# Hybrid decoder layer: the mixer's last convolution tile taken ahead of the recurrence's input, eight of its taps on ScalarE and GpSimd, gating and output products by channel halves

## The chip, the cores and the metric

The kernel runs on one core of a Trainium2 chip. The metric is the device time of one execution in microseconds (us). A core has five engines that work side by side and meet through semaphores: TensorE (PE, matrix products into PSUM, with PEld its weight loads), VectorE (DVE), ScalarE (ACT), GpSimd (POOL) and SyncE (SP, which issues most DMAs). Each works through its own queue in order.

## The reference

One decoder layer for 512 tokens of width 1024, all in float32. A half step of a SwiGLU network stands on either side of a token mixer:

```python
x = x + 0.5 * ffn1(rmsnorm(x))
x = x + mixer(rmsnorm(x))
x = x + 0.5 * ffn2(rmsnorm(x))
return rmsnorm(x)
```

The mixer makes four parts of 512 channels from one projection. Two of them feed a convolution branch, two a linear recurrence, and one output projection takes both:

```python
c_val, c_gate, r_x, r_gate = split(h @ w_in)
u  = silu(layernorm(depthwise_conv(c_val * sigmoid(c_gate), width=31)))
xr = depthwise_conv(r_x, width=4)
r, i = sigmoid(blockdiag(xr, w_a)), sigmoid(blockdiag(xr, w_x))
a  = exp(-8 * r * softplus(-lam))
y  = scan(a, sqrt(1 - a * a) * i * xr) * gelu(r_gate)      # h[t] = a[t] h[t-1] + b[t]
return concat([u, y]) @ w_out
```

## The kernel before

Every product is made of three in a fast 32-bit format: each operand is split into a high and a low part, and high x high, high x low and low x high are added in PSUM. So a product of 128 output channels for 512 tokens over a width of 1024 is 24 matmuls of 128x512 (`mm_feat`, L294).

The program is written as a list of units (`Unit`, L66): slabs of weights, a piece of TensorE work (`mm`), and what empties its accumulators (`evac`). `run` (L239) walks the list, loads and splits the slabs a few units ahead, issues `mm`, advances side work by an estimate of the time passed, and issues `evac`. Side work stands in generators: `chains` (norms, the recurrence `lru`, `layernorm`), `convs` (convolution taps on VectorE) and `pool_convs` (on ScalarE and GpSimd). `need(key)` advances them until a result is there. The tile framework then orders each engine's queue by priority and program order; `tc.keep_in_program_order` (called `pin` here) fixes an instruction's place.

The mixer's 512 channels per part are four tiles of 128 on the partitions, with the tokens along the free dimension. Its units on TensorE, in order:

- `zc_units(c)` for convolution tiles 0, 1 and 2 (gate product, value product; the sigmoid and the multiplication leave the input in `ub`),
- `rx_units`: the recurrence's input, four tiles; `evac` makes the four-tap convolution on ScalarE and VectorE (L728 to L733), the last one starts `lru`,
- `zc_units(3)`, then `rg_units`: the recurrence's gate branch, four tiles, emptied by a GELU (L755) that asks for the key `roots` first,
- `out_units`: the output projection. It first takes the recurrence's half y (slabs `sy`; t is a tile of 128 tokens) for t = 0, 1, 2, asks for the LayerNorm's variance (`need("var")`), takes y for t = 3, and then the convolution's half u (slabs `su`).

A convolution tile has 31 taps. Tiles 0, 2 and 3 are on VectorE (`conv_dve`, L642): one instruction per tap, alternately into two PSUM banks, and an add of the two at the end. Tile 1 is on ScalarE, which makes a scaled copy per tap, and GpSimd, which adds the copies in pairs (`conv_pool`, L662). When a tile is done, TensorE sums it over the channels with a matrix of ones (`channel_sum`, L629, into `pm`); after the fourth, `layernorm` subtracts the mean, squares (ScalarE), sums again on TensorE, takes root and reciprocal, and makes SiLU and the split of u.

`lru` (L765): eight block-diagonal gate products on TensorE (L771, into `pga`), eight sigmoids (L772), GpSimd multiplies input by gate (L777), ScalarE makes tanh, exp and squares (L781 to L786), VectorE combines (L789), ScalarE takes the root (L793), GpSimd multiplies it in (L794), VectorE scans the four tiles (L801). Then it waits until all four GELU tiles are there and no VectorE convolution is left (L804), multiplies y by the gate in two halves of two tiles (L808), and splits it (L809, L810); `done["y"]` lets the output products start.

ScalarE's activation functions sit in tables; a switch between some of them puts an `ACT_TABLE_LOAD` into its queue. Weights of the following network are split by ScalarE (`S.copy`, L202) into one of five `hl` buffers, where the slabs `sy` lay before.

Of the kernel before, what the change touches and what calls it, by code (L numbers as in the profile page):

```python
# [29 lines left out]
TAPS = 31  # L30
PR_NORM = 800
# [40 lines left out]
def layer_kernel(ctx: ExitStack, tc, x, gains, w_g1, w_u1, w_d1a, w_d1b, w_in,  # L72
# [519 lines left out]
    def zc_units(c, parts):  # L592
# [12 lines left out]
        def val_out(t0, n):  # L605
            V.tensor_mul(mx["ub"][:, c, 30 + t0:30 + t0 + n], box["v"][:, :n], box["s"][:, :n])
# [35 lines left out]
    def conv_dve(c):  # L642
        acc, o = [bank("pc"), bank("pc")], conv_out(c)
        for j in range(TAPS):
# [7 lines left out]
            else:  # L652
                V.scalar_tensor_tensor(out=o if j == TAPS - 2 else to, in0=src,  # L653
# [3 lines left out]
        V.tensor_add(o, acc[0], o)  # L657
        yield 0.66
        conv_done(c)


    def conv_pool(c):  # L662
# [16 lines left out]
        conv_done(c)  # L679

    def layernorm():
# [33 lines left out]
        done["u"] = (hi, lo)  # L715
# [28 lines left out]
    def rg_units():  # L744
# [7 lines left out]
        def evac(c):  # L752
# [3 lines left out]
            if c == 3:  # L756
                done["gl"] = True
# [7 lines left out]
    def lru():  # L765
        xr, r, i_, th = lr["xr"], two("r"), two("i"), two("th")
        for c in range(4):
            at = (slice(None), c % 2, slice(None))
            for gi, (to, b) in enumerate(((r, P_BA), (i_, P_BX))):
                pga = bank("pga")  # L770
                PE.matmul(pga, bd[:, gi, c, :], xr[c // 2][at], start=True, stop=True)  # L771
# [3 lines left out]
        pin = tc.keep_in_program_order  # L775
# [3 lines left out]
        for c in range(4):  # L779
            at = (slice(None), c % 2, slice(None))  # L780
            S.activation(th[c // 2][at], r[c // 2][at], AF.Tanh, scale=psp[:, c:c + 1])  # L781
        for c in range(4):
            at = (slice(None), c % 2, slice(None))
            S.activation(r[c // 2][at], r[c // 2][at], AF.Exp, scale=nsp[:, c:c + 1])
# [14 lines left out]
        for c in range(4):  # L799
            at = (slice(None), c % 2, slice(None))  # L800
            pin(V.tensor_tensor_scan(th[c // 2][at], r[c // 2][at], xr[c // 2][at],  # L801
                                     0.0, ALU.mult, ALU.add))
# [4 lines left out]
        for q in range(2):  # L807
            pin(V.tensor_mul(th[q], th[q], lr["gl"][q]))  # L808
            S.copy(hi[q], th[q])  # L809
            V.tensor_sub(lo[q], th[q], hi[q].bitcast(F32))  # L810
            dve(2.4)
        done["y"] = (hi, lo)


    def out_units(after):
# [13 lines left out]
        def part(ts, slabs, key, first, cs=range(4), halves=(0, 1)):  # L829
            hi, lo = need(key)  # L830
            for t in ts if first else ():
                box[t] = [bank("po") for _ in range(2)]
            for t in ts:
                for oh in halves:
                    for c in cs:
                        at = (slice(None), c % 2, toks(t))
# [253 lines left out]
```

## Time and profile before

| | before |
|---|---|
| three runs, median (lowest to highest) | 880.58 us (879.61 to 880.58) |
| the profiled execution, its own time | 884.38 us |
| its span | 882.4 us |
| busy in the span: PE, PEld | 853.7 us, 767.0 us |
| DVE, ACT, POOL | 612.5, 413.3, 90.0 us |
| granted TensorE clock, mean | 0.989 |
| mixer in the span: its first input product, first output product on y, on u | 368.29, 476.98, 505.52 us |

The profile is one execution under the hardware profiler, with times from the start of its span; it took 3.8 us longer than the median of the runs. A row of a timeline has the start, the duration, the engine, the source line, the operation, output tile<-input tiles, shape and count, and in brackets the idle time before it with what ended it. A float32 product of ones shows as two matmul records for one instruction. The ends of matmuls are modelled.

### The profile page before, as it was taken

How to read it: one execution, taken by the hardware profiler on the slowest of the kernel's cores; microseconds unless marked ns; L12 is line 12 of the kernel's file. 1: busy time of each engine (PE TensorE's matmuls, PEld its weight loads, DVE VectorE, ACT ScalarE, POOL GpSimd, SP SyncE). 2: the span in 40 equal slices, each digit the busy share in tenths (PEclk: the TensorE clock that was granted, in tenths of full speed). 3: DMA queues.
4: the chain of work that ended last, by engine and by line, in shares of the span. 5: the costliest groups of instructions: out<-in, count | busy, mean ns of one | idle time of the engine just before them, and what ended most of it. 6: DMA issues, size and time to landing. Idle time of an engine off the chain costs nothing.

```text
span 882.4 us, 13317 instructions
## 1 busy us (share of the span) xinstructions
PE 853.7 (97%) x5388; PEld 767.0 (87%) x5388; DVE 612.5 (69%) x854; ACT 413.3 (47%) x647; POOL 90.0 (10%) x112
## 2 busy tenths in 40 slices
PE   7999998999998999999996999999999999999996
PEld 5999987999888998898783789999889999899985
DVE  5999665987667863659988569587547775558644
ACT  7666433646434652426652535455225554235523
POOL 2000011000011001208830010000000000000001
PEclk9999999999999999999997999999999999999999
DMA  7543688364788389655442021234312324223402
GB/s 280 166 168 106 233 286 311 139 215 167 228 306 301 97 268 404 234 214 192 143 151 88 4 92 64 82 105 131 123 49 97 127 89 164 76 72 97 143 1 95
DMA packets 36719, 139.10 MB, mean 158 GB/s; under 512 B 5041, under 2 KB 5169, under 8 KB 33970
## 3 DMA queue, kind: packets, MB, share of 16 engines
q1 hardware_dynamic: 29170, 112.04, 37.8%
q0 software_dynamic: 6912, 25.17, 7.2%
q10 hardware_dynamic: 576, 1.05, 0.3%
q8 instruction: 42, 0.69, 0.3%
q14 instruction: 19, 0.16, 0.1%
HBM read 110.98 MB, written 27.26 MB: 157 GB/s over the span
## 4 chain that ended last, share of the span: by engine, by line
PE 70%; issue 15%; DVE 5%; DMA 5%; ACT 4%; POOL 1%; SPq 0%; POOLq 0%; ACTq 0%; DVEq 0%
PE px L308 17%; PE pz L308 8%; PE pz L299 7%; PE pd L515 5%; PE pd L516 5%; PE pd L514 5%; PE pgate L299 5%; PE pup L299 5%; PE pw L308 4%; DVE pc L653 2%; DMA sraw<-in_w_out 2%; DMA raw<-in_w_u 2%; PE po L514 1%; PE po L516 1%; PE po L515 1%
## 5 line engine op out<-in xcount | busy, mean ns | idle before, releaser
L211 DVE TENSOR_TENSOR hl<-raw,hl 128x1024 fp32r<-128x1024 f32 (+1 forms) x132 | 142.5, 1083 | 58.3 <-ACT hl L202 44.1
L514 PE MATMUL pd<-hl,act 128*128 128x512 f32 x304 | 118.5, 390 | 0.0
L515 PE MATMUL pd<-hl,act 128*128 128x512 f32 x304 | 118.4, 389 | 0.0
L516 PE MATMUL pd<-hl,act 128*128 128x512 f32 x304 | 118.3, 389 | 0.0
L308 PE MATMUL px<-sx,hl 128*128 128x256 f32 x816 | 108.4, 283 | 5.6 <-ACT sg L467 5.6
L211 DVE TENSOR_TENSOR hl<-tt,hl 128x1024 fp32r<-128x1024 f32 x68 | 82.9, 1219 | 38.5 <-ACT hl L237 37.1
L308 PEld LDWEIGHTS px<-sx,hl 128*128 128x128 f32 x816 | 101.7, 192 | 6.2 <-ACT sg L467 6.2
L308 PE MATMUL pz<-sx,hl 128*128 128x256 f32 x816 | 106.1, 279 | 0.0
L308 PEld LDWEIGHTS pz<-sx,hl 128*128 128x128 f32 x816 | 99.8, 189 | 0.0
L202 ACT CAST hl<-raw 128x1024 fp32r<-128x1024 f32 x64 | 66.5, 1053 | 63.1 <-PE pd L516 47.7
L308 PE MATMUL px<-h_hi,hl 128*128 128x256 f32 x544 | 85.6, 280 | 0.0
L237 ACT CAST hl<-tt 128x1024 fp32r<-128x1024 f32 x68 | 71.6, 1053 | 28.7 <-PE pd L516 18.4
L237 ACT CAST hl<-raw 128x1024 fp32r<-128x1024 f32 x68 | 56.8, 836 | 41.0 <-PE pd L516 29.2
L308 PEld LDWEIGHTS px<-h_hi,hl 128*128 128x128 f32 x544 | 74.2, 188 | 1.2
L516 PEld LDWEIGHTS pd<-hl,act 128*128 128x128 f32 x304 | 57.1, 188 | 11.9
L514 PEld LDWEIGHTS pd<-hl,act 128*128 128x128 f32 x304 | 57.1, 188 | 11.6
L515 PEld LDWEIGHTS pd<-hl,act 128*128 128x128 f32 x304 | 57.1, 188 | 11.5
L299 PE MATMUL pz<-h_hi,hl 128*128 128x512 f32 (+1 forms) x320 | 64.9, 352 | 0.0
L299 PEld LDWEIGHTS pz<-h_hi,hl 128*128 128x128 f32 x320 | 51.8, 188 | 9.2 <-issue 1.9
L653 DVE SCALAR_TENSOR_TENSOR pc<-sx,ch,pc 128x512 f32<-128x512 f32 x84 | 56.9, 749 | 0.0
L288 DVE TENSOR_TENSOR slo<-sraw,shi 128x1024 fp32r<-128x1024 f32 x24 | 29.4, 1223 | 36.0 <-ACT shi L287 36.0
L287 ACT CAST shi<-sraw 128x1024 fp32r<-128x1024 f32 x24 | 25.2, 1051 | 53.4 <-DMA sraw<-in_w_in 32.3
(181 smaller groups left out, 1397.5 us busy)
## 6 DMA issues: line engine op xcount, KB each, us to landing
raw<-in_w_g SPq DMA_DIRECT2D x44, 512.0 KB, 3.5
raw<-in_w_u SPq DMA_DIRECT2D x44, 512.0 KB, 3.8
hl<-wsi SPq DMA_DIRECT2D x16, 1024.0 KB, 4.8
sraw<-in_w_in SPq DMA_DIRECT2D x16, 512.0 KB, 5.8
wsi<-shi POOLq DMA_DIRECT2D x16, 512.0 KB, 5.5
wsi<-slo POOLq DMA_DIRECT2D x16, 512.0 KB, 5.6
raw<-in_w_d1a SPq DMA_DIRECT2D x16, 512.0 KB, 3.6
raw<-in_w_d2a SPq DMA_DIRECT2D x16, 512.0 KB, 3.5
```

Source lines behind the costliest of these rows:

```text
L202: S.copy(s.hi, s.raw)
L211: V.tensor_sub(s.lo, s.raw, s.hi.bitcast(F32))
L237: S.copy(s.hi, s.raw)
L287: S.copy(hi, raw)
L288: V.tensor_sub(lo, raw, hi.bitcast(F32))
L299: PE.matmul(ps, w[:, k, :], h[:, k, t0:t0 + n], start=(i == 0 and k == 0), stop=(i == 2 and k == KT - 1))
L308: PE.matmul(ps[:, 0:HT], w[:, k * P:(k + 1) * P], h[:, k, :], start=(first and i == 0 and k == 0), stop=(i == 2 and k == 3), skip_group_ch ...
L514: PE.matmul(ps, ahi, whi, start=first, stop=False)
L515: PE.matmul(ps, ahi, wlo, start=False, stop=False)
L516: PE.matmul(ps, alo, whi, start=False, stop=last)
L653: V.scalar_tensor_tensor(out=o if j == TAPS - 2 else to, in0=src, scalar=par(c, P_DW + j), in1=to, op0=ALU.mult, op1=ALU.add)
```

## The change

Four things change, all in the mixer.

1. The units of tile 3 of the convolution (`zc_units(3)`) stand before `rx_units` and no longer behind them.
2. Tile 3's last eight taps (23 to 30) leave VectorE. `conv_part` makes eight scaled copies on ScalarE and four adds on GpSimd; `conv_dve` makes 23 taps, waits for the key `part`, and adds that sum.
3. The recurrence scans, gates and splits its output by halves of two channel tiles. The gate of a half needs only that half's GELU tiles (`gl0`, `gl1`), and the condition that no convolution is left is gone. Sigmoids, tanhs and exps are pinned in program order, the subtraction that makes the low part too.
4. The output products on y for t = 0, 1, 2 come by halves: first tiles 0 and 1 for the three t, then tiles 2 and 3. Their keys are `y0`, `y1`, and `u0`, `u1` for the other branch.

```diff
-                else:
-                    convs.append(conv_dve(c))
+                elif c == 3:
+                    pool_convs.append(conv_part(c, range(TAPS - PART, TAPS)))
+                    convs.append(conv_dve(c, TAPS - PART, "part"))
+                else:
+                    convs.append(conv_dve(c, TAPS))
...
-        V.tensor_add(o, acc[0], o)
+        V.tensor_add(o, acc[taps % 2], o)
         yield 0.66
+        if rest is not None:
+            while rest not in done:
+                yield 0.3
+            V.tensor_add(o, o, done[rest])
+            yield 0.66
         conv_done(c)
...
+    def conv_part(c, taps):
+        acc = slot([P, 2, T], "ca")
+        for j in taps[::2]:
+            to = acc if j == taps[0] else slot([P, 2, T], "cm")
+            for i in range(2):
+                S.activation(to[:, i, :], mx["ub"][:, c, j + i:j + i + T], AF.Copy,
+                             scale=par(c, P_DW + j + i))
+            if j > taps[0]:
+                G.tensor_add(acc, acc, to)
+                yield 2.5
+        G.tensor_add(acc[:, 0, :], acc[:, 0, :], acc[:, 1, :])
+        yield 1.25
+        done["part"] = acc[:, 0, :]
...
-                S.activation(to[c // 2][at], pga, AF.Sigmoid, bias=par(c, b))
+                pin(S.activation(to[c // 2][at], pga, AF.Sigmoid, bias=par(c, b)))
...
-        for c in range(4):
-            at = (slice(None), c % 2, slice(None))
-            pin(V.tensor_tensor_scan(th[c // 2][at], r[c // 2][at], xr[c // 2][at],
-                                     0.0, ALU.mult, ALU.add))
-            dve(1.2)
-        while "gl" not in done or convs:
-            yield 1
         hi, lo = two("yhi", F32R), two("ylo", F32R)
         for q in range(2):
+            for c in range(2):
+                at = (slice(None), c, slice(None))
+                pin(V.tensor_tensor_scan(th[q][at], r[q][at], xr[q][at], 0.0, ALU.mult, ALU.add))
+                dve(1.2)
+            yield 1
+        for q in range(2):
+            while f"gl{q}" not in done:
+                yield 1
             pin(V.tensor_mul(th[q], th[q], lr["gl"][q]))
             S.copy(hi[q], th[q])
-            V.tensor_sub(lo[q], th[q], hi[q].bitcast(F32))
+            pin(V.tensor_sub(lo[q], th[q], hi[q].bitcast(F32)))
             dve(2.4)
-        done["y"] = (hi, lo)
+            done[f"y{q}"] = (hi[q], lo[q])
...
-        out_ = [Unit(sy, 5.44, lambda t=t: part((t,), sy, "y", True)) for t in range(3)]
+        out_ = [Unit(sy[2 * q:2 * q + 2], 2.72, lambda q=q, t=t: part((t,), sy, True, (2 * q, 2 * q + 1)))
+                for q in range(2) for t in range(3)]
...
-    u += rx_units() + zc_units(3, [ALL]) + rg_units()
+    u += zc_units(3, [ALL]) + rx_units() + rg_units()
```

What the framework made of it stands in the queues. In the rows below a name has its tile's number behind it, a line number is that of the kernel concerned, and `x8` counts equal instructions.

TensorE, where the gate products stand before: the last of them, then tile 3's value product (`pz_4372`), then the first product of the gate branch (`pz_4425`) with the sum of tile 1 (`pm_4180<-cv_3963`) near its end.

```order
L771 MATMUL pga_4358<-xr_4105,bd 128x512
L299 MATMUL pz_4372<-h_hi,hl_4152 128x512 x8
L299 MATMUL pz_4372<-h_lo,hl_4152 128x512 x8
L299 MATMUL pz_4372<-h_hi,hl_4152 128x512 x8
L299 MATMUL pz_4425<-h_hi,hl_4204 128x512 x8
L299 MATMUL pz_4425<-h_lo,hl_4204 128x512 x8
L299 MATMUL pz_4425<-h_hi,hl_4204 128x512 x6
L633 MATMUL pm_4180<-cv_3963,ones 128x512
```

TensorE in the changed kernel: the last matmuls of the third recurrence input, the fourth (`pz_4349`), the sum of tile 1, the first product of the gate branch (`pz_4398`), and then the gate products (`pga_4429` on).

```order
L300 MATMUL pz_4298<-h_hi,hl_4102 128x512 x8
L300 MATMUL pz_4349<-h_hi,hl_4146 128x512 x8
L300 MATMUL pz_4349<-h_lo,hl_4146 128x512 x8
L300 MATMUL pz_4349<-h_hi,hl_4146 128x512 x8
L637 MATMUL pm_4174<-cv_3963,ones 128x512
L300 MATMUL pz_4398<-h_hi,hl_4196 128x512 x8
L300 MATMUL pz_4398<-h_lo,hl_4196 128x512 x8
L300 MATMUL pz_4398<-h_hi,hl_4196 128x512 x8
L797 MATMUL pga_4429<-xr_4198,bd 128x512
```

The gate products moved behind one more product and behind the sum of tile 1, which stood behind them.

VectorE before: the end of tile 2 (`cv_4184`), tile 3's input (L606), the recurrence's pair of combinations (L789), and then tile 3's first tap.

```order
L657 TENSOR_TENSOR cv_4184<-pc_4182,cv_4184 128x512
L606 TENSOR_TENSOR sx_464_3727<-pz_4372,sgc_4368 128x512
L789 SCALAR_TENSOR_TENSOR th_4331<-i_4329,th_4331 128x1024
L789 SCALAR_TENSOR_TENSOR th_4332<-i_4330,th_4332 128x1024
L647 TENSOR_SCALAR pc_4487<-sx_464_3727,ch 128x512
```

VectorE in the changed kernel, at that pair (L814): thirteen taps of tile 3 (`pc_4457`, `pc_4458`) stand ahead of it, the last two of which are shown, and ten behind it; then come the scans (L828), the first half's gating (L834), and the two adds that end tile 3 (L661, L666).

```order
L657 SCALAR_TENSOR_TENSOR pc_4458<-sx_464_3727,ch,pc_4458 128x512
L657 SCALAR_TENSOR_TENSOR pc_4457<-sx_464_3727,ch,pc_4457 128x512
L814 SCALAR_TENSOR_TENSOR th_4427<-i_4425,th_4427 128x1024
L814 SCALAR_TENSOR_TENSOR th_4428<-i_4426,th_4428 128x1024
L657 SCALAR_TENSOR_TENSOR pc_4458<-sx_464_3727,ch,pc_4458 128x512
...
L828 SCALAR_TENSOR_TENSOR th_4427<-r_4423,xr_4198 128x512 x2
L828 SCALAR_TENSOR_TENSOR th_4428<-r_4424,xr_4199 128x512 x2
L834 TENSOR_TENSOR th_4427<-th_4427,gl_4396 128x1024
L661 TENSOR_TENSOR cv_4178<-pc_4458,cv_4178 128x512
L666 TENSOR_TENSOR cv_4178<-cv_4178,ca_4334 128x512
```

The pair moved from ahead of tile 3 to its middle, and the first half's gating from behind tile 3's last add to ahead of it.

ScalarE before, in LayerNorm: the root of the variance (L696), the table for SiLU, SiLU and cast of u (L707, L708), and then the first cast of the following network's weights (L202).

```order
L696 ACTIVATE rs_4660<-pm_4645,lneps 128x512
L707 ACT_TABLE_LOAD
L707 ACTIVATE cv_3963<-cv_3963,ch 128x256 x2
L708 CAST uhi_4688<-cv_3963 128x256 x2
L707 ACTIVATE cv_4184<-cv_4184,ch 128x256 x2
L708 CAST uhi_4689<-cv_4184 128x256 x2
...
L202 CAST hl_4802<-raw_4568 128x1024
```

ScalarE in the changed kernel, at the same place.

```order
L720 ACTIVATE rs_4709<-pm_4682,lneps 128x512
L203 CAST hl_4811<-raw_4594 128x1024
L203 CAST hl_4813<-raw_4596 128x1024
L203 CAST hl_4815<-raw_4655 128x1024
L731 ACT_TABLE_LOAD
L731 ACTIVATE cv_3963<-cv_3963,ch 128x256 x2
L732 CAST uhi_4723<-cv_3963 128x256 x2
```

Three casts of weights moved from behind u to ahead of it. TensorE's sum of tile 3 moved too: before, it stood ahead of the first output product; now it stands behind 68 of the 72 products on y for t = 0, 1, 2, with the variance sums right behind those, ahead of y for t = 3.

More of the change, by code (lines that the diff above doesn't have):

```diff
@@ L30 @@
 TAPS = 31
+PART = 8
 PR_NORM = 800
@@ L639, in conv_done, with conv_dve @@
             chains.append((PR_LN, layernorm()))
-    def conv_dve(c):
+    def conv_dve(c, taps, rest=None):
         acc, o = [bank("pc"), bank("pc")], conv_out(c)
-        for j in range(TAPS):
+        for j in range(taps):
             src, to = mx["ub"][:, c, j:j + T], acc[j % 2]
@@ L652, in conv_dve @@
             else:
-                V.scalar_tensor_tensor(out=o if j == TAPS - 2 else to, in0=src,
+                V.scalar_tensor_tensor(out=o if j == taps - 1 else to, in0=src,
                                        scalar=par(c, P_DW + j), in1=to,
@@ L714, in layernorm @@
             dve(1.6)
-        done["u"] = (hi, lo)
+        for q in range(2):
+            done[f"u{q}"] = (hi[q], lo[q])
     lr = {}
@@ L755, in evac @@
                 S.activation(lr["gl"][c // 2][:, c % 2, :], lr["g", c], AF.Gelu_apprx_tanh))
-            if c == 3:
-                done["gl"] = True
+            if c % 2:
+                done[f"gl{c // 2}"] = True
         out_ = []
@@ L780, in lru @@
             at = (slice(None), c % 2, slice(None))
[L781 removed]
+            pin(S.activation(th[c // 2][at], r[c // 2][at], AF.Tanh, scale=psp[:, c:c + 1]))
         for c in range(4):
             at = (slice(None), c % 2, slice(None))
[L784 removed]
+            pin(S.activation(r[c // 2][at], r[c // 2][at], AF.Exp, scale=nsp[:, c:c + 1]))
         for q in range(2):
@@ L827, in out_units, with part @@
         box = {}
-        def part(ts, slabs, key, first, cs=range(4), halves=(0, 1)):
-            hi, lo = need(key)
-            for t in ts if first else ():
+        def part(ts, slabs, first, cs=range(4), halves=(0, 1)):
+            for t in ts if first and cs[0] == 0 else ():
                 box[t] = [bank("po") for _ in range(2)]
@@ L835, in part @@
                     for c in cs:
+                        hi, lo = need(f"{'y' if first else 'u'}{c // 2}")
                         at = (slice(None), c % 2, toks(t))
-                        mm_tok(box[t][oh], hi[c // 2][at], lo[c // 2][at],
+                        mm_tok(box[t][oh], hi[at], lo[at],
                                slabs[c].hi[:, cols(oh)], slabs[c].lo[:, cols(oh)],
@@ L849, in fin_two @@
                     fin(t, oh)
-        out_ = [Unit(sy, 5.44, lambda t=t: part((t,), sy, "y", True)) for t in range(3)]
+        out_ = [Unit(sy[2 * q:2 * q + 2], 2.72, lambda q=q, t=t: part((t,), sy, True, (2 * q, 2 * q + 1)))
+                for q in range(2) for t in range(3)]
         out_ += [Unit([], 0.0, lambda: need("var"))]
-        out_ += [Unit(sy, 5.44, lambda: part((3,), sy, "y", True))]
-        out_ += [Unit(su, 2.72, lambda c=c: part((0, 1), su, "u", False, (c,)),
+        out_ += [Unit(sy, 5.44, lambda: part((3,), sy, True))]
+        out_ += [Unit(su, 2.72, lambda c=c: part((0, 1), su, False, (c,)),
                       fin_two if c == 3 else None) for c in range(4)]
-        out_ += [Unit(su, 2.72, lambda t=t, oh=oh: part((t,), su, "u", False, halves=(oh,)),
+        out_ += [Unit(su, 2.72, lambda t=t, oh=oh: part((t,), su, False, halves=(oh,)),
                       lambda t=t, oh=oh: fin(t, oh)) for t in (2, 3) for oh in range(2)]
```

3 lines of the change are left out of this document (2 added, 1 removed).

## The prediction

> **What bounds the kernel now.** I read the profile's page, then TensorE's timeline through the mixer, the clock by windows, and the timelines of the engines that TensorE waits for there.
>
> ```profile
> span 882.4 us, 13317 instructions
> PE 853.7 (97%) x5388; PEld 767.0 (87%) x5388; DVE 612.5 (69%) x854; ACT 413.3 (47%) x647; POOL 90.0 (10%) x112
> ```
>
> TensorE (PE) is busy for 97% of the span, so a change in the mixer is worth what it does to holes in TensorE's row and to its clock. The timeline (start, duration, engine, line, operation, count, in brackets the idle time before and who ended it):
>
> ```profile
> 431.68 7.03 PE L771 MATMUL pga<-xr,bd 128*128 128x512 f32 x16
> 438.14 2.40 PE L299 MATMUL pz<-h_hi,hl 128*128 128x512 f32 x8
> 449.00 1.02 PE L633 MATMUL pm<-cv,ones 128*128 128x512 f32 x2
> 466.68 1.04 PE L299 MATMUL pz<-h_hi,hl 128*128 128x512 f32 x2
> 474.77 2.08 PE L633 MATMUL pm<-cv,ones 128*128 128x512 f32 x2 [7.06 <-DVE cv L657]
> 476.98 0.80 PE L514 MATMUL po<-hl,yhi 128*128 128x512 f32 x1
> 482.90 0.50 PE L514 MATMUL po<-hl,yhi 128*128 128x512 f32 x1 [0.96 <-ACT yhi L809]
> 483.71 3.60 PE L633 MATMUL pm<-sq,ones 128*128 128x512 f32 x8
> 487.38 0.40 PE L514 MATMUL po<-hl,yhi 128*128 128x512 f32 x1
> 505.52 0.39 PE L514 MATMUL po<-hl,uhi 128*128 128x512 f32 x1
> ```
>
> The input products end at 467.7 and the first output product (L514) starts at 476.98: one hole of 9.3 us with a lone sum (L633) in it, then 0.96 us at 482.90. From 487.38 on there is no hole: 80 products to 505.52, 0.227 us each. The windows (PE's granted clock stands ahead of the DMA share, third from the right) show what the hole does to the clock:
>
> ```profile
> 468.00:471.00 3.00, 0.00 (x0) 0.00 (x0) 3.00 (x6) 0.34 (x1) 0.00 (x0) 0.99 0.78 235
> 471.00:475.00 4.00, 0.23 (x1) 0.23 (x2) 3.97 (x7) 0.00 (x0) 0.00 (x0) 0.50 0.21 86
> 479.00:480.80 1.80, 1.80 (x6) 1.43 (x5) 1.80 (x4) 0.00 (x0) 0.00 (x0) 0.50 0.00 0
> 480.80:482.00 1.20, 1.14 (x4) 0.57 (x3) 0.91 (x1) 0.20 (x1) 0.00 (x0) 0.84 0.00 0
> ```
>
> It halves about 3.3 us after the last product and is whole again at about 481.2, so the products from 476.98 to 481.2 lose half of 4.2 us, 2.1 us. All that could be won here is 9.3 - 0.9 (the sum, at 0.9 of full speed) + 1.0 + 2.1 = 11.5 us. What ends the hole is VectorE (DVE):
>
> ```profile
> 444.28 0.69 DVE L606 TENSOR_TENSOR sx<-pz,sgc 128x512 f32<-128x512 f32 x1 [2.50 <-PE pz L299]
> 446.24 2.36 DVE L789 SCALAR_TENSOR_TENSOR th<-i,th 128x1024 f32<-128x1024 f32 x2 [1.27 <-ACT i L786]
> 453.83 5.03 DVE L801 TENSOR_TENSOR_SCAN th<-r,xr 128x512 f32<-128x512 f32 x4
> 458.79 13.89 DVE L653 SCALAR_TENSOR_TENSOR pc<-sx,ch,pc 128x512 f32<-128x512 f32 x21
> 474.03 0.69 DVE L657 TENSOR_TENSOR cv<-pc,cv 128x512 f32<-128x512 f32 x1
> 474.63 1.22 DVE L808 TENSOR_TENSOR th<-th,gl 128x1024 f32<-128x1024 f32 x1
> ```
>
> A tap costs 13.89 / 21 = 0.66 us. Channel tile 3 gets its input only at 444.28, and its taps fill VectorE until the gating (L808).
>
> **The change part by part.** *Tile 3 ahead, eight taps away, gates later.* VectorE loses 8 x 0.66 = 5.3 us and gains one add of 0.6 us, and tile 3's input comes 30 us earlier. But the four recurrence inputs and their gate products (L771) now come later on TensorE. Three products of 24 matmuls each take 16.38 us, one 5.46:
>
> ```profile
> 415.46 16.38 PE pz L299 x72
> ```
>
> At 431.68, where the gate products stood, the fourth recurrence input begins and ends at 437.1. Behind it the order has the sum of tile 1 (before: at 449.00, amid a later product), which needs GpSimd's last add:
>
> ```profile
> 429.13 8.64 POOL L675 TENSOR_TENSOR ca<-ca,cm 128x1024 f32<-128x1024 f32 x4 [3.10 <-ACT cm L673]
> 437.85 1.29 POOL L677 TENSOR_TENSOR cv<-ca 128x512 f32<-128x512 f32 x1
> ```
>
> GpSimd waits there for copies that ScalarE (ACT) makes behind an evacuation at 426.49 (below); the evacuation at that place of the new order ends the same product by count, so 439.1 stands and TensorE waits 2.0 us. With the sum (0.9) and one product the gate products start at 445.6, 13.9 later than 431.68. That is the price of the new order, and it meets this chain on ScalarE:
>
> ```profile
> 426.49 0.75 ACT L728 ACTIVATE px<-pz,ch 128x512 f32<-128x512 f32 x1 [3.00 <-PE pz L299]
> 427.64 2.57 ACT L673 ACTIVATE cm<-sx,ch 128x512 f32<-128x512 f32 x4
> 439.43 1.95 ACT L781 ACTIVATE th<-r,psp 128x512 f32<-128x512 f32 x3
> 441.40 1.28 ACT L784 ACT_TABLE_LOAD   x1
> 445.16 2.00 ACT L786 ACTIVATE i<-r 128x1024 f32<-128x1024 f32 x2
> 475.88 1.04 ACT L809 CAST yhi<-th 128x1024 fp32r<-128x1024 f32 x1 [7.54 <-DVE th L808]
> 487.35 0.69 ACT L696 ACTIVATE rs<-pm,lneps 128x512 f32<-128x512 f32 x1 [1.10 <-PE pm L633]
> 491.79 1.28 ACT L707 ACT_TABLE_LOAD   x1 [3.75 <-DVE cv L706]
> 493.09 1.10 ACT L707 ACTIVATE cv<-cv,ch 128x256 f32<-128x256 f32 x2
> 494.09 0.70 ACT L708 CAST uhi<-cv 128x256 fp32r<-128x256 f32 x2
> 503.68 3.90 ACT L202 CAST hl<-raw 128x1024 fp32r<-128x1024 f32 x4 [4.09 <-PE po L516]
> ```
>
> From gate products to VectorE's first L789 it takes 446.24 - 431.68 = 14.6 us (sigmoids, tanh, table load, exp, squares), the pair done at 448.6. Sigmoids pinned ahead of all tanhs add 0 to 0.6 (one 0.65 tanh stood in a gap). So the pair runs from 460.4 to 462.8. In VectorE's new order ten of tile 3's 23 taps stand behind it. The thirteen ahead of it are 8.6 us of work after tile 2. That one ends at about 444: VectorE's queue has tile 3's input behind tile 2's first tap, so all else of tile 2 waits some 3 us for that product, which ends near 415 (the row at 415.46 begins behind it); 30 taps and 12 recurrence taps follow, 42 x 0.66 + 0.6 = 28.3. Even begun 5 us late (their accumulator bank waits for a gate's sigmoid) they end by 458: VectorE waits for ScalarE, and that wait eats the taps saved. Then 10 x 0.66 + 5.0 (scans) + 1.2 (gating) + 1.0 (cast) = 13.8: the first output product starts at 476.7, against 476.98: **-0.3 us**, bounds -1.5 (an L789 1.2 sooner, the cover of its 2.5 us idle gone) and +1.5. TensorE has run dry at 445.6 + 6.5 + 3 x 5.46 + 0.9 = 469.4, so the hole is 7.3 us and the clock halves as before.
>
> *Eight taps on ScalarE and GpSimd.* Eight copies of 0.64 (2.57 / 4) lie in ScalarE's gaps, and four GpSimd adds, 3 x 2.4 (9.93 / 4 for the row at 429.13 and its end) + 1.3 = 8.5 us, stand ahead of GpSimd's multiplications for the recurrence. One add waits for a copy behind the first sigmoid, so they end near 452, and the multiplications at 457. The squares, at 445.16 + 13.9 = 459.1, want them no sooner. Nothing. The slabs' loads on SP's queue move with their products, in the order in which TensorE reads them; none of the rows above has it waiting for a DMA. Nothing.
>
> *Halves.* The wait at 482.90 goes (-1.0): 36 products on the first half run while VectorE and ScalarE make the second, ready near 481 (add 1.3, subtraction 1.2, gating 1.2, cast 1.0 behind 475.7, and a pause). The clock's recovery costs 2.1 as before; with the resumption at another moment, 1.7 to 3.2 (half of 6.4, 474.77 to 481.2).
>
> *Sum of tile 3, LayerNorm.* Before, that sum lay in the hole and LayerNorm ran under 80 products. Now it stands behind 68 products: 476.7 + 68 x 0.227 + 2.1 = 494.2, done at 495.2. The rest goes by these rows:
>
> ```profile
> 478.10 2.48 DVE L687 TENSOR_TENSOR cv<-cv,pm 128x512 f32<-128x512 f32 x4
> 488.07 3.37 DVE L702 RECIPROCAL rs<-rs 128x256 f32<-128x256 f32 x2 [3.96 <-ACT rs L696]
> 491.35 2.70 DVE L706 TENSOR_TENSOR cv<-cv,rs 128x256 f32<-128x256 f32 x8
> ```
>
> Subtractions to 497.8, last square 498.6, last variance sum 499.6, root (L696) to 500.5, reciprocals to 503.9, first product 504.3. TensorE meanwhile has only the fourth token tile's 24 products, 499.6 to 505.1. And in ScalarE's new order three casts of the next weights (L202) stand between the root and the SiLU. They overwrite the slabs that those very products read: before, such a cast waited 4.09 us for the last of them. The first slab is free after 15 products, at 503.2; three casts (3.90 / 4 each) to 506.2; table 507.5; two SiLUs 508.5; cast 508.9. **Second hole: 505.1 to 509.0, 3.9 us**; without casts in front it would be 504.3 + 2.7 = 507.0, 1.9 us.
>
> The first product on u starts at 509.0 against 505.52: **+3.5 us**, bounds +1 and +7, and TensorE has no hole behind it to give that back. The profiled execution's own 884.38 would become 887.9; on the median of the runs, 880.58, that is 884.1.
>
> *The clock in the second hole.* The windows have it halve 3.3 us after the last product, so 3.9 us lie at the edge; if it halves, 1.7 to 3.2 us more are lost. [...] Its 3.3 us taken for a fixed delay would make the sum +6, which is the first rival.
>
> **The rivals.** *The clock halves again*: for it the 3.3 us; against it that the second hole exceeds that by just 0.6. 884.1 + 2.4 = 886.5; chance 0.25. *Not slower, the second hole closes*: decided on ScalarE between root and SiLU; if u's first half is cast by 505.1 the first u product comes at 505.1, 0.4 ahead of before: 880.2, or 878.6 with the better bound of the first hole (1.2 more) and of the clock (0.4). It needs 3.9 us, of which the casts hold 2.0 and the variance chain 1.9; against it speaks that ScalarE takes its queue in order. Same 0.09, faster 0.07. *GpSimd late*: if its adds delay the recurrence's multiplications past the roots, which follow the pair's end at 462.8, the scans slip. The slack is some 6 us; two adds of 2.4 more would fit in it, four would cost 3.6 and give 887.7. The copies that feed the adds stand among ScalarE's evacuations, which speaks for it; the rate of the rows against it. 0.08. *The change doesn't do what it says*: the products do start on the first half alone and tile 3 is ahead, as the order shows; what doesn't follow is that the hole closes. It is the forecast itself: +3.5 us, 884.1, chance 0.51.
>
> **The numbers.** About 0.2%, 1.8 us, is what a measurement of this kernel can tell from no change. Slower: 0.51 + 0.25 + 0.08 = 0.84, of which 0.02 goes to "same" for the forecast's lower bound: 0.82. Same 0.11, faster 0.07. The range goes from 881.6 (+1) to 887.9 (3.5, the clock's 3.2, and 0.6 of the first hole's bound of 1.5): it holds the slower rivals and leaves out the others, 0.16, and the farthest ends.
>
> **Right or wrong.** Right: TensorE waits about 2 us for GpSimd ahead of the sum near 437, has a hole of 7 to 8 us that ends near 477 with ScalarE's cast, and one of 3 to 5 us ended by the cast of u; VectorE waits for the squares (now L811) with taps behind. Wrong: a first output product ahead of 475, or no idle time ahead of the first product on u.

## The result, and the profile after

The changed kernel took 887.68 us (median of 7 runs, 883.96 to 890.45) beside 880.58 us (7 runs, 878.54 to 884.74) of the kernel before: a ratio of 1.0066, 95% interval 1.0038 to 1.0094. It is 5.8 us slower (3.3 to 8.3). By the two medians alone it is 7.1 us. The forecast, 884.1 us, was 3.5 us above before: it had the sign, and 2.3 us are missing from it by the ratio, 3.6 by the medians. The measured median lies just inside the stated range, which ends at 887.9.

```profile
span 884.4 us, 13329 instructions
PE 851.4 (96%) x5388; PEld 764.2 (86%) x5388; DVE 607.0 (69%) x847; ACT 418.1 (47%) x655; POOL 98.3 (11%) x116
```

The profiled execution took 886.39 us. Its span is only 2.0 us longer than that of before, since its mixer began at 363.66 us and that of before at 368.29. Part of this is that in the execution of before the clock was half for two windows of 3.41 us in the first network (at 150.09 and 276.39 us), which the change doesn't touch; at half clock each costs up to 1.7 us, half of its length. So positions below count from the mixer's first input product.

TensorE's timeline in the changed kernel, at the places that the prediction named:

```profile
434.58 1.13 PE L637 MATMUL pm<-cv,ones 128*128 128x512 f32 x2 [1.93 <-POOL cv L686]
435.14 3.93 PE L300 MATMUL pz<-h_hi,hl 128*128 128x512 f32 x8
442.61 7.03 PE L797 MATMUL pga<-xr,bd 128*128 128x512 f32 x16
473.35 0.80 PE L515 MATMUL po<-hl,yhi 128*128 128x512 f32 x1 [6.46 <-ACT yhi L835]
490.47 1.02 PE L637 MATMUL pm<-cv,ones 128*128 128x512 f32 x2
492.99 3.70 PE L637 MATMUL pm<-sq,ones 128*128 128x512 f32 x8 [0.57 <-ACT sq L716]
505.85 0.50 PE L515 MATMUL po<-hl,uhi 128*128 128x512 f32 x1 [3.69 <-ACT uhi L732]
```

All three waits are where they were forecast: for GpSimd's sum of tile 1 (1.93 us, forecast 2.0), for the cast of y (6.46, forecast 7.3), for the cast of u (3.69, forecast 3.9). The wait at the second half of y is gone. The first output product, at 473.35 in this span, lies 109.7 us behind the mixer's start, which is 478.0 on the scale of before; so it is not the one ahead of 475 that the prediction named as a sign of being wrong. VectorE, ScalarE and GpSimd show the reasons:

```profile
446.49 0.81 DVE L651 TENSOR_SCALAR pc<-sx,ch 128x512 f32<-128x512 f32 x1 [5.98 <-ACT r L798]
457.68 2.36 DVE L814 SCALAR_TENSOR_TENSOR th<-i,th 128x1024 f32<-128x1024 f32 x2 [2.48 <-ACT i L811]
466.54 4.57 DVE L828 TENSOR_TENSOR_SCAN th<-r,xr 128x512 f32<-128x512 f32 x4
491.53 2.48 DVE L711 TENSOR_TENSOR cv<-cv,pm 128x512 f32<-128x512 f32 x4 [13.31 <-PE pm L637]
500.73 2.70 DVE L730 TENSOR_TENSOR cv<-cv,rs 128x256 f32<-128x256 f32 x8
```

```profile
500.15 2.94 ACT L203 CAST hl<-raw 128x1024 fp32r<-128x1024 f32 x3 [2.74 <-PE po L517]
503.11 1.28 ACT L731 ACT_TABLE_LOAD   x1
504.41 1.09 ACT L731 ACTIVATE cv<-cv,ch 128x256 f32<-128x256 f32 x2
505.41 0.70 ACT L732 CAST uhi<-cv 128x256 fp32r<-128x256 f32 x2
```

```profile
433.25 1.27 POOL L686 TENSOR_TENSOR cv<-ca 128x512 f32<-128x512 f32 x1
447.88 1.27 POOL L701 TENSOR_TENSOR ca<-ca 128x512 f32<-128x512 f32 x1
```

VectorE stands 5.98 us (tile 3's accumulator bank comes free with a sigmoid, L798) and 2.48 us (squares, L811) with taps of tile 3 in its queue, and 13.31 us for tile 3's sum, which TensorE takes behind 68 products on y. Then ScalarE does three weight casts ahead of SiLU.

What the prediction did not have is in the windows. In the profiles of before and of the changed kernel all seven changes of the granted clock lie on a grid of 3.413 us, from 150.09 to 880.55 us and from 435.63 to 882.77 us, so the windows are cut on that grid (behind the comma TensorE's busy time comes first, and the granted clock stands third from the right):

```profile
432.22:435.63 3.41, 1.48 (x5) 0.58 (x4) 3.41 (x6) 1.88 (x3) 3.33 (x3) 1.00 0.51 154
435.63:439.05 3.42, 3.42 (x10) 2.64 (x9) 3.42 (x7) 0.00 (x0) 3.34 (x2) 0.50 0.39 158
439.05:442.46 3.41, 3.41 (x17) 2.81 (x16) 1.42 (x3) 0.00 (x0) 0.26 (x1) 1.00 0.00 0
500.49:503.90 3.41, 1.67 (x8) 1.05 (x6) 3.41 (x10) 3.39 (x4) 0.00 (x0) 1.00 0.00 0
503.90:507.31 3.41, 1.46 (x6) 1.24 (x7) 2.56 (x4) 3.40 (x9) 0.00 (x0) 1.00 0.49 154
507.31:510.73 3.42, 3.42 (x9) 2.65 (x8) 2.67 (x6) 3.42 (x10) 0.00 (x0) 0.50 0.57 175
```

A window in which TensorE was busy for 1.48 us is followed by one at half clock, and so is one with 1.46; one with 1.67 is not. The half clock comes when TensorE is already back at work: each time 10 matmuls (9 at the second place) fill a window that takes 17 at full clock, 1.7 us lost. The window ahead was not idle throughout either time: TensorE stood for some 1.9 us of its 3.41.

The profile of before holds two such places in its first network, behind waits of 2.63 and 2.83 us:

```profile
149.64 2.56 PE L308 MATMUL px<-sx,hl 128*128 128x256 f32 x12 [2.63 <-ACT sg L467]
146.68:150.09 3.41, 0.78 (x6) 0.57 (x6) 3.33 (x5) 2.59 (x5) 1.55 (x3) 1.00 0.90 364
150.09:153.50 3.41, 3.41 (x19) 3.41 (x18) 3.41 (x5) 1.26 (x2) 0.05 (x1) 0.50 0.63 249
276.28 2.00 PE L308 MATMUL px<-sx,hl 128*128 128x256 f32 x8 [2.83 <-ACT sg L467]
272.97:276.39 3.42, 0.58 (x6) 0.38 (x5) 3.25 (x5) 2.57 (x5) 1.21 (x3) 1.00 1.02 417
276.39:279.80 3.41, 3.41 (x17) 3.41 (x18) 3.41 (x5) 0.75 (x3) 0.39 (x1) 0.50 0.71 281
```

Both waits are shorter than the 3.3 us that the prediction took from the mixer's hole, so the profile on which it was made already shows that less than that is enough.

### The profile page after: what moved, and what is told of

Read it like the earlier page. It is cut to its first block, busy times and chain, and to the rows that moved or that the text cites. A ratio compares the mean times of both kernels' runs of the same rounds, so it can differ in the third digit from the quotient of the medians.

```text
span 884.4 us, 13329 instructions
## 1 busy us (share of the span) xinstructions
PE 851.4 (96%) x5388; PEld 764.2 (86%) x5388; DVE 607.0 (69%) x847; ACT 418.1 (47%) x655; POOL 98.3 (11%) x116
## 4 chain that ended last, share of the span: by engine, by line
PE 45%; ACT 3%; DVE 3%; issue 1%; POOL 0%; POOLq 0%; ACTq 0%; DVEq 0%
PE px L309 11%; PE pz L309 5%; PE pd L516 3%; PE pd L517 3%; PE pd L515 3%; PE pgate L300 3%; PE pup L300 3%; PE pw L309 3%; PE po L515 2%; PE po L516 1%; PE po L517 1%; PE pdl L516 1%; PE pdl L517 1%; PE pdl L515 1%; DVE pc L657 1%
## 5 line engine op out<-in xcount | busy, mean ns | idle before, releaser
L212 DVE TENSOR_TENSOR hl<-raw,hl 128x1024 fp32r<-128x1024 f32 (+1 forms) x132 | 142.6, 1082 | 56.1 <-ACT hl L203 41.4
L309 PE MATMUL px<-sx,hl 128*128 128x256 f32 x816 | 106.5, 280 | 4.4 <-ACT sg L468 4.4
L309 PEld LDWEIGHTS px<-sx,hl 128*128 128x128 f32 x816 | 99.9, 189 | 5.0 <-ACT sg L468 5.0
L309 PEld LDWEIGHTS px<-h_hi,hl 128*128 128x128 f32 x544 | 74.3, 189 | 1.2
L657 DVE SCALAR_TENSOR_TENSOR pc<-sx,ch,pc 128x512 f32<-128x512 f32 x76 | 51.7, 749 | 0.0
```

The lines of the kernel that those rows point to most:

```text
L212: V.tensor_sub(s.lo, s.raw, s.hi.bitcast(F32))
L309: PE.matmul(ps[:, 0:HT], w[:, k * P:(k + 1) * P], h[:, k, :], start=(first and i == 0 and k == 0), stop=(i == 2 and k == 3), skip_group_ch ...
L657: V.scalar_tensor_tensor(out=o if j == taps - 1 else to, in0=src, scalar=par(c, P_DW + j), in1=to, op0=ALU.mult, op1=ALU.add)
```

## The experiments

The theories. **U**: the new order of units costs the time, since the gate products, and with them the recurrence, come some 14 us later. **T**: the eight taps on ScalarE and GpSimd cost it. **H**: the halves cost it, since tile 3's sum now stands behind the y products and the LayerNorm starts late. The table has all runs; "gates", "y", "u" are the starts of the first gate product and the first products on y and u, "end" that of the span, in us from the mixer's first input product in the profiled execution.

| run | ratio to before, 95% | gates | y | u | end |
|---|---|---|---|---|---|
| before | 1 | 63.4 | 108.7 | 137.2 | 514.1 |
| changed kernel | 1.0066 (1.0038 to 1.0094) | 79.0 | 109.7 | 142.2 | 520.8 |
| e2_units_alone | 1.0088 (1.0062 to 1.0114) | 79.0 | 117.0 | 145.5 | 522.9 |
| e15_taps_alone | 1.0057 (1.0037 to 1.0077) | 63.4 | 111.3 | 141.0 | 517.8 |
| e3_halves_alone | 0.9948 (0.9927 to 0.9969) | 63.4 | 99.3 | 131.0 | 510.2 |
| e1_old_units (taps, halves) | 1.0052 (1.0032 to 1.0072) | 63.4 | 100.9 | 137.5 | 516.6 |
| e13_no_halves (units, taps) | 1.0020 (0.9992 to 1.0048) | 77.4 | 109.5 | 138.0 | 514.9 |
| e3_taps_back (units, halves) | 1.0103 (1.0081 to 1.0125) | 77.4 | 108.1 | 142.6 | 522.8 |
| e5_sum1_later | 1.0057 (1.0031 to 1.0083) | 74.3 | 105.0 | 138.5 | 518.2 |
| e7_sum3_front | 1.0017 (0.9992 to 1.0042) | 77.4 | 108.1 | 137.1 | 513.9 |
| e12_casts_late | 1.0027 (1.0010 to 1.0044) | 77.4 | 108.1 | 139.8 | 517.7 |
| e14_front_nowait | 0.9958 (0.9938 to 0.9978) | 74.3 | 105.0 | 133.4 | 510.9 |
| e9_old_front | 0.9964 (0.9943 to 0.9986) | 63.4 | 101.0 | 132.4 | 509.3 |
| e4_halves_sum_front | 0.9904 (0.9868 to 0.9939) | 63.4 | 99.3 | 128.2 | 505.0 |

From the first product on u to the last it takes 23.3 to 23.4 us in these profiles, or 25.0 to 26.2 where the clock is half in between; the last one lies 353.5 to 354.5 us ahead of the end in all of them.

**The old order, the rest of the change kept (e1_old_units).**

```diff
-    u += zc_units(3, [ALL]) + rx_units() + rg_units()
+    u += rx_units() + zc_units(3, [ALL]) + rg_units()
```

> The changed kernel with the units in the old order (recurrence input, then tile 3); taps on ScalarE and GpSimd and the halves stay. Theory U (the new order of units costs the time: it puts the gate products some 14 us later): the gate products come when they came before, the first half of y no longer waits for tile 3, and the first hole (9.3 us before, 6.5 after) shrinks below 1.5 us; the hole ahead of u (3.69 us) stays, since the sum of tile 3 still lies behind the y products. About 6 us faster than the kernel before (4 to 8). Theory T (the eight taps on ScalarE and GpSimd cost it: GpSimd's sums and the accumulator bank of tile 3 come late): the loss stays, 3 to 7 us slower than before. Theory H (the halves cost it, through the late sum of tile 3): the loss shrinks only by what the first hole gives.

It was 0.52% slower than before. The gates came in time and the first hole shrank to 1.51, 1.95 and 0.85 us, as U says, but y was only 7.8 us earlier and u not at all. The reason stood on VectorE and GpSimd, here their groups between 436 and 480 us (VectorE) and 430 and 480 us (GpSimd): busy time and mean ns of one behind the bar.

```profile
L828 DVE TENSOR_TENSOR_SCAN th<-r,xr 128x512 f32<-128x512 f32 x4 | 11.5, 2925 | 0.0
L834 DVE TENSOR_TENSOR th<-th,gl 128x1024 f32<-128x1024 f32 x2 | 3.4, 1718 | 0.0
```

```profile
L699 POOL TENSOR_TENSOR ca<-ca,cm 128x1024 f32<-128x1024 f32 x3 | 9.7, 3232 | 0.2
L684 POOL TENSOR_TENSOR ca<-ca,cm 128x1024 f32<-128x1024 f32 x3 | 7.1, 2375 | 3.3 <-ACT cm L682 3.1
```

The scans, 1314 ns each before, took 2925, and GpSimd's adds for tile 3 (L699) 3232, against 2375 for those of tile 1 (L684): in the old order scans and adds fall together. So do the first half's gating (L834) and GpSimd's last add. U alone does not carry, and a fourth theory, **C**, came up: VectorE's scans and GpSimd's adds get in each other's way.

**The new order alone, in the kernel before (e2_units_alone)** (the same two lines the other way round, nothing else).

> The kernel before with only the units of tile 3 put ahead of the recurrence's input; no taps moved, no halves. Theory U: gate products some 15 us later with TensorE's 2 us wait for GpSimd ahead of them, all of tile 3's taps beyond the pair still ahead of the gating; first hole 11 to 13 us instead of 9.3, and y some 7 us later: 7 us slower than before (4 to 10). Theories T and H: this part is harmless or a gain, between 3 us faster and 1 us slower.

```profile
436.59 1.62 PE L633 MATMUL pm<-cv,ones 128*128 128x512 f32 x2 [1.92 <-POOL cv L677]
480.43 2.08 PE L633 MATMUL pm<-cv,ones 128*128 128x512 f32 x2 [11.50 <-DVE cv L657]
```

0.88% slower, 7.8 us, as U has it: the wait for GpSimd is there, and the wait ahead of tile 3's sum is 11.50 us where it was 7.06. The first hole, up to y, is so 13.7 us instead of 9.3, more than U's 11 to 13.

**The eight taps alone, in the kernel before (e15_taps_alone)**, to test C where little but the taps differs (the pins on sigmoids, tanhs and exps stay from the change):

```diff
+                elif c == 3:
+                    pool_convs.append(conv_part(c, range(TAPS - PART, TAPS)))
+                    convs.append(conv_dve(c, TAPS - PART, "part"))
```

> The kernel before with only the eight taps of tile 3 on ScalarE and GpSimd: old order, gating behind tile 3, products on y by all four tiles. Theory C: GpSimd's adds run beside the scans, which take 2.5 to 3 us each instead of 1.3; that eats the 4.7 us that VectorE saves, the first hole stays at 8 to 10 us: within 2 us of the kernel before. If the taps were simply saved: first hole 4 to 5 us, 4 to 6 us faster than the kernel before.

```profile
L826 DVE TENSOR_TENSOR_SCAN th<-r,xr 128x512 f32<-128x512 f32 x4 | 12.1, 3087 | 0.0
```

```profile
472.98 2.07 PE L637 MATMUL pm<-cv,ones 128*128 128x512 f32 x2 [9.68 <-DVE cv L666]
```

0.57% slower, 5 us, more than C's 2; the first hole, up to y, is 11.9 us, not 8 to 10. VectorE gave up 5.3 us of taps, took on an add of 0.7, and paid 7.1 us more for four scans (12.1 against 5.0); so y came 2.6 us later. The taps are no gain there but a loss.

**The halves alone, in the old order with all taps on VectorE (e3_halves_alone).**

```diff
-                elif c == 3:
-                    pool_convs.append(conv_part(c, range(TAPS - PART, TAPS)))
-                    convs.append(conv_dve(c, TAPS - PART, "part"))
...
-    u += zc_units(3, [ALL]) + rx_units() + rg_units()
+    u += rx_units() + zc_units(3, [ALL]) + rg_units()
```

> Old order of units, all 31 taps of tile 3 on VectorE, and the halves with the late sum: part 3 and 4 of the change alone. Theory C (in the run with the old order and the eight taps away, the four scans took 2.9 us each instead of 1.3 while GpSimd's adds ran beside them at 3.2 instead of 2.4 us; the two engines get in each other's way): without those adds the scans go back to 1.2 to 1.4 us each, the first half of y is there when the input products end, the first hole is under 2 us; the hole ahead of u stays at 3 to 5 us with a half clock behind it. 5 to 8 us faster than the kernel before. Theory H (what the first hole gives, the late sum and the hole ahead of u take back, whatever the scans do): within 2 us of the kernel before. Rival: the scans were slow for another reason that stays; then 3 to 5 us slower as in that run.

```profile
L825 DVE TENSOR_TENSOR_SCAN th<-r,xr 128x512 f32<-128x512 f32 x4 | 5.1, 1315 | 0.0
```

```profile
496.10 0.64 PE L515 MATMUL po<-hl,uhi 128*128 128x512 f32 x1 [3.69 <-ACT uhi L729]
```

0.52% faster (4.6 us, just under the bound). Without GpSimd's adds a scan takes 1315 ns again, and TensorE goes from the input products into y with no wait. Against e1_old_units, from which only the eight taps differ, that is 1.04%, 9 us. ScalarE's copies, the other thing that the eight taps bring, are not what slows the scans: in e1_old_units the last scan, from 461.64 on, takes 3.34 us, and from 462 to 465 GpSimd is busy with its adds for 2.92 us and ScalarE not at all. C is shown. The hole ahead of u, 3.69 us, is the same as in the changed kernel, which has another order and other taps: it belongs to the halves (H).

**Tile 3's sum in front (e7_sum3_front in the changed kernel; e4_halves_sum_front in the halves alone; e9_old_front in the old order with the eight taps).** The same edit three times; `conv_done` sets the key.

```diff
+        done[f"conv{c}"] = True
...
+        out_.insert(0, Unit([], 0.0, lambda: need("conv3")))
```

> The changed kernel, but the output products are asked for only once tile 3 is done, so that its sum stands ahead of the y products on TensorE and not behind 68 of them; LayerNorm then runs beside y. Theory U with H as its second part: the hole ahead of u (3.69 us) and the half clock behind it (1.7 us) go, the first hole stays within 1 us: 5 us faster than the changed kernel (3.5 to 6.5), about 1 us slower to 1 us faster than before. Rival (the second hole is the three weight casts ahead of SiLU, not the place of the sum): casts still stand ahead, hole of 2 us or more stays, at most 2 us won. Second rival: waiting for tile 3 makes the first hole longer by what it takes from the second: no change.

> As the run with the halves alone (old order, all taps on VectorE), but output products are asked for only once tile 3 is done, so that TensorE's order has tile 3's sum among the first y products and not behind 68 of them. If the late sum makes the hole ahead of u: that hole (3 to 5 us) and the half clock behind it (1.7 us) go; 8 to 11 us faster than the kernel before, 3 to 5 faster than the halves alone. Two waits of about 2 us, for tile 3 and for a square, may stay and one may halve the clock. If the three weight casts ahead of SiLU make it: the hole keeps 2 us or more, and no more than 2 us are won over the halves alone.

> Old order, the eight taps on ScalarE and GpSimd, halves, and tile 3's sum among the first y products: the run before this one with the eight taps added. If the two engines get in each other's way, scans of 2.5 to 3 us and GpSimd adds of 3.2 us come back, y is 5 to 7 us later, and it is 1 to 4 us faster than the kernel before, slower than the same without the taps moved by 5 or more. If they do not, the eight taps save VectorE 4 us ahead of tile 3's sum and this is the fastest of all, 11 us faster than the kernel before.

In all three the wait for u is gone and the first product on u comes earlier than without the edit, by 5.1, 2.8 and 5.0 us. Of the 5.1 us, 1.6 are the half clock at the wait for GpSimd, which the profile of e7_sum3_front doesn't have. e7_sum3_front won 0.49% on the changed kernel, e4_halves_sum_front 0.44% on the halves alone, as expected, though in both pairs the intervals overlap; y did not come later. The edit moves the three weight casts behind SiLU too, since SiLU is ready earlier, so it does not part sum and casts. TensorE in e4_halves_sum_front has two waits left:

```profile
477.35 1.12 PE L634 MATMUL pm<-cv,ones 128*128 128x512 f32 x2 [0.80 <-DVE cv L659]
479.92 3.70 PE L634 MATMUL pm<-sq,ones 128*128 128x512 f32 x8 [1.44 <-ACT sq L714]
```

With 873.63 us it beats both kernels: 0.9904 of before. e9_old_front, the same with the eight taps, has scans of 2934 ns and is 0.60% slower than it: C again. But y came only 1.7 us later than there, where 5 to 7 were expected; u came 4.3 us later.

**SiLU ahead of the weight casts (e12_casts_late).** The LayerNorm is asked for up to u where only its variance was, and SiLU's cast and the weight casts are pinned.

```diff
-        out_ += [Unit([], 0.0, lambda: need("var"))]
+        out_ += [Unit([], 0.0, lambda: need("u1"))]
...
-                S.copy(o, v)
+                tc.keep_in_program_order(S.copy(o, v))
...
+            if "u1" in done:
+                tc.keep_in_program_order(cast)
```

> The changed kernel, with SiLU and the cast of u ahead of the three weight casts in ScalarE's order; the sum of tile 3 stays behind 68 of the y products. If the casts hold part of the second hole, as the prediction has it (2.0 of 3.9 us): the hole ahead of u shrinks from 3.69 to 1.5 to 2 us and the clock stays whole behind it: 2 to 4 us faster than the changed kernel, about 2 us slower than before. If the place of the sum alone sets it: no change against the changed kernel.

```profile
505.11 0.50 PE L517 MATMUL po<-hl,uhi 128*128 128x512 f32 x1 [1.74 <-ACT uhi L734]
```

```profile
434.67:438.09 3.42, 1.83 (x6) 1.24 (x7) 3.42 (x6) 1.63 (x3) 3.34 (x3) 1.00 0.77 271
438.09:441.50 3.41, 3.41 (x16) 2.80 (x16) 3.38 (x6) 0.00 (x0) 2.85 (x2) 1.00 0.11 41
502.94:506.35 3.41, 1.67 (x7) 1.05 (x7) 2.46 (x8) 3.40 (x8) 0.00 (x0) 1.00 0.00 0
506.35:509.76 3.41, 3.41 (x16) 2.82 (x15) 1.52 (x4) 3.41 (x10) 0.00 (x0) 1.00 0.00 0
```

The hole is 1.74 us: the casts held 1.95 of 3.69, the late sum the rest. With 1.67 us of work in its window the clock stays whole here. And at the wait for GpSimd, 1.94 us long here as well, the grid cuts it so that no window has less than 1.83 us of work: no half clock there either. The ratio is 0.39% below that of the changed kernel, about what was expected; the two intervals meet, so the size stands on the trace.

**Tile 1's sum later (e5_sum1_later), and with tile 3's sum in front (e14_front_nowait).** `conv_pool` sets `tile1` instead of calling `conv_done`; the second kernel has the edit above as well.

```diff
-        conv_done(c)
+        done["tile1"] = True
...
+            if c == 0:
+                need("tile1")
+                conv_done(1)
             need("roots")
```

> The changed kernel, but TensorE's sum of tile 1 is asked for only behind the first product of the gate branch, so nothing on TensorE waits for GpSimd's last add ahead of the gate products. Theory U with the clock: the 1.93 us wait goes, and the half clock that followed it (1.7 us) too; the recurrence and all behind it come 3.6 us earlier: 3.6 us faster than the changed kernel (2.5 to 5), about 2 us slower than before. If the wait cost its own length alone: 2 us faster than the changed kernel. Rival: the recurrence waits for something else (GpSimd's multiplications, tile 3's accumulator bank), and the hole ahead of y takes up what is won: no change against the changed kernel.

> The changed kernel with two repairs: tile 1's sum behind the first gate branch product, and tile 3's sum among the first y products. If the new order had no other price than the wait for GpSimd and the late sum: as fast as the run with the halves alone and the sum in front in the old order, 8 us faster than the kernel before. Theory U (the gate products still come 10 us later, and the recurrence is the chain that ends the first hole): a first hole of 5 to 6 us with a half clock behind it stays, 1 to 4 us faster than the kernel before.

Alone, the edit moved gates and y 4.7 us ahead in the trace (1.6 of it the half clock at the wait) and u 3.7 us; then its clock was half for two windows behind the hole ahead of u, one in the changed kernel, and 2.5 us are left at the end. In the times it is 0.09%, which the intervals don't resolve; 3.6 us had been expected. With tile 3's sum in front, the same edit is worth 0.59% (e7_sum3_front to e14_front_nowait, intervals apart). That kernel is 0.42% faster than before, and what U says is left of the new order stands in its timeline:

```profile
467.61 0.80 PE L515 MATMUL po<-hl,yhi 128*128 128x512 f32 x1 [5.59 <-ACT yhi L839]
```

y comes 5.7 us later than in e4_halves_sum_front (105.0 against 99.3), and the end 5.9. e4_halves_sum_front has all taps on VectorE, too, but in the new order that changes nothing at y, as the next runs show.

**The halves undone (e13_no_halves) and the taps put back (e3_taps_back), each in the changed kernel.** The first has the scans, gating and y products of the kernel before, still with separate keys; the second lacks the `elif c == 3` above.

> The changed kernel with the halves undone: new order and eight taps stay, all four scans come first, the gating waits for the taps of tile 3 and the y products take all four tiles. Theory U with H: the 1.93 us wait with its half clock stays (3.6 us), the first hole is 7 to 9 us and the wait for the second half comes back (1 to 2 us), the hole ahead of u is gone: 2 to 5 us slower than the kernel before, a little faster than the changed kernel; the halves lose in it. Theory T (eight taps cost it): as the changed kernel or slower. If the halves are a gain in the new order: 8 us slower than the kernel before, or more.

> The changed kernel with all 31 taps of tile 3 on VectorE (units and halves of the change alone). If the eight taps were worth next to nothing there, since VectorE waits for the squares with taps behind them: within 1.5 us of the changed kernel, at most 2 slower. If they were what keeps the change from being worse: 4 us slower than the changed kernel or more. Theory T (the copies and GpSimd's adds of the eight taps delay the recurrence): 2 us faster than the changed kernel or more.

Without the halves the changed kernel is 0.46% faster (the intervals just meet): in the new order they lose, in the old one they win 0.52%. Of their price u shows 4.2 us (142.2 against 138.0), 1.6 of them the half clock at the wait for GpSimd, which that profile doesn't have. With the taps back it is 0.37% slower, 3.3 us where at most 2 were expected (intervals overlap). y comes no later in that trace: 108.1, as in e7_sum3_front and e12_casts_late, which have the taps moved; the 109.7 of the changed kernel has the half clock in it. u comes 0.4 us later, though y is 1.6 earlier, after a longer wait for a square (1.44 us against 0.57) and a half clock behind the first hole that ends 5.8 us after the first product on y instead of 3.2. The end is 2.0 us later, since the clock behind the hole ahead of u was half for 6.83 us, and for 3.41 in the changed kernel. So by the trace the taps' own worth in the new order is under 1 us, and what the times show beyond it is not told apart from the clock.

## Why the prediction was right or wrong

- **Right: the new order.** Gate products at +13.9 from the start of the mixer. In the four executions of that order with the wait and a whole clock they lay at 77.4, 14.0 behind the 63.4 of before; in the profiled changed kernel 15.6.
- **Right: the first hole doesn't close.** Forecast for y -0.3 us; 108.1 in e12_casts_late against 108.7, -0.6, with a whole clock, and +1.0 with the half one. VectorE waits for the squares with taps behind, and this eats the taps saved, as argued. The hole itself is 6.46 us and not 7.3, in e7_sum3_front and e12_casts_late as well: there the input products end 0.5 us later than forecast and y starts 0.3 earlier.
- **Right: the second hole and its makers.** 3.69 us against 3.9, and the casts' share of 2.0 was 1.95.
- **Right where the change puts them: eight taps cost nothing.** GpSimd's adds end at 449.15 us (L701) and the scans begin at 466.54. That adds could meet scans was not considered, and in the old order it decides.
- **Wrong in size: the term for the wait for GpSimd.** It was summed as 2.0 us of idle time. It measured 1.93 and took a half clock with it, 1.6 more, in this execution; four others with the same wait kept the whole clock (e7_sum3_front, e12_casts_late, e13_no_halves, e3_taps_back).
- **Failed: the step "The clock in the second hole".** It took 3.3 us after the last product as what halves the clock, and the forecast counts nothing for the clock behind a hole of 3.9 us. No run shows that such a hole leaves the clock whole: all five profiles with the 3.69 us hole (the changed kernel, e1_old_units, e3_halves_alone, e5_sum1_later, e3_taps_back) have a half clock behind it, for 3.41 or 6.83 us. In the windows less than 1.5 us of work was enough for it, and the profile of before had two such places, behind waits of 2.63 and 2.83 us; the prediction reckoned with one hole alone. The rival "The clock halves again", given 0.25, is what happened: 886.5 us by its sum, 886.4 by the measured ratio (880.58 x 1.0066). That the two agree so well is partly luck: the rival had one half clock of 2.4 us, and the trace has 1.7 there and 1.6 at the wait for GpSimd.

The sum by trace, against before: y -0.6, half clock at the wait +1.6, from y to u +4.0, half clock behind u +1.7, together the 6.7 us measured from the mixer on. Forecast were -0.3, 0, +3.8 and 0. With tile 3's sum in front the changed kernel is no longer told apart from before (1.0017, 0.9992 to 1.0042): the late sum, with the casts behind it and the half clock, is what makes it slower. The new order is why nothing was won to set against it: in the old one the halves gain 0.52%.

Runs of one kernel differ by several us, and the granted clock has a part in that: of the changed kernel's seven runs the fastest (883.96 us) has a mean of 0.991 and the slowest (890.45 us) 0.984. Over the 190 runs on record, each against the mean of its kernel beside it, 0.01 less of clock goes with some 8 us more, which takes up two fifths of the spread. That the grid cuts the same waits another way each time would do this; where the half clocks lie is known for the profiled runs alone, so it stays open.

## What to carry to other kernels

Price a wait of TensorE by where it falls in the windows of the granted clock, not by its length alone: here, behind sixteen of sixteen windows at whole clock with less than 1.5 of 3.41 us of work, the clock was half, so a wait of 1.9 us cost 3.6 in the changed kernel and 1.9 in e7_sum3_front, and one of 3.7 brought the drop in five profiles of five. Before work goes to GpSimd, look at which VectorE instructions run beside it, not only at whether GpSimd has room: here scans went from 1.3 to 2.9 us. When a result is asked for sooner, look at what loses its place in the queue by that: in the new order the late sum of tile 3 cost more than the halves won.

## What the runs showed of the hardware

- The clock: its changes lie on a grid of 3.413 us in the profiles of before and of the changed kernel. From 30 us into the span on, these two have eight windows at whole clock with less than 1.5 us of TensorE work (before 0.78, 0.58, 0.18 and, at the end, 0; the changed kernel 1.48, 0.54, 1.46 and, at the end, 0), and behind every one of them the clock is half. Behind their next fullest, 1.52 us at 875.95, 1.67 at 500.49 and 1.74 at 145.50 in the changed kernel and 1.70 at 873.72 in before, it is whole. Eight windows of other profiles with less than 1.5 us have the half clock behind them too: 1.49 us in e2_units_alone, 1.45 in e9_old_front, 1.08 in e3_taps_back, 0.74 and 0 in e1_old_units, 0.60 and 0 in e5_sum1_later, 0.21 in e3_halves_alone. With 1.7 us both happened: in e15_taps_alone, where TensorE waits for 1.74 of the 3.41 us from 476.64 on, its matmuls lie 0.43 us apart from 480.05 on; 1.67 us at 502.94 in e12_casts_late and 1.70 at 429.71 in e7_sum3_front have the whole clock behind them, and so have the five with 1.83 to 2.85 us (e12_casts_late, e13_no_halves, e3_taps_back). A stretch of 3.41 us with 1.47 us of work from 476.85 on in e4_halves_sum_front has it as well; that its ends lie on the grid of that execution is not shown. The same wait of 1.92 us, whole in one window or cut by two:

```profile
433.67:437.08 3.41, 1.49 (x6) 0.79 (x5) 2.68 (x5) 1.26 (x2) 2.71 (x3) 1.00 0.34 98
437.08:440.49 3.41, 3.41 (x8) 2.31 (x7) 3.41 (x6) 0.00 (x0) 0.00 (x0) 0.50 0.51 214
```

```profile
429.71:433.13 3.42, 1.70 (x6) 1.09 (x7) 3.42 (x6) 1.77 (x3) 3.34 (x3) 1.00 0.76 263
433.13:436.54 3.41, 3.41 (x17) 2.80 (x16) 3.41 (x6) 0.00 (x0) 2.98 (x2) 1.00 0.13 48
```

  The first two rows are of e2_units_alone, the others of e7_sum3_front. Windows at half clock with 2.52 (e5_sum1_later), 2.87 (before) and 3.1 us of work (e13_no_halves) had the next one at half as well; behind 2.98 (e1_old_units) and 3.24 (the changed kernel) it was whole.
- VectorE and GpSimd: scans, with both inputs in SBUF, took 2.9 to 3.1 us on the mean beside GpSimd's adds (2925 ns in e1_old_units, 2934 in e9_old_front, 3087 in e15_taps_alone) and 1.2 to 1.3 without (1206 in the changed kernel, 1314 in before, 1315 in e3_halves_alone); the adds 3.2 (3232 to 3235) and 2.4 (2367 in the changed kernel). Taps, which read one operand from PSUM, were not slowed: eleven in the changed kernel, beside GpSimd's multiplications, took 0.67 us each, against 0.66 in before, and one between the scans of e1_old_units, amid the adds, 0.72, where a lone one of the changed kernel took 0.75 (436.40):

```profile
447.87 7.33 DVE L657 SCALAR_TENSOR_TENSOR pc<-sx,ch,pc 128x512 f32<-128x512 f32 x11
449.10 4.78 POOL L802 TENSOR_TENSOR xr<-xr,i 128x1024 f32<-128x1024 f32 x2
```

  No run shows what makes the difference between scans and taps. A scan and an add side by side took less time than one after the other would: 3.3 us (the last scan of e1_old_units, 3.34, and its adds, 3.23 each) against 1.3 + 2.4.
